# Six joints of a transformer block's kernel reordered, the recurrence's largest decays computed by ACT with the reference as bias, and one branch's matmuls dealt out along the last head

## The chip, the cores and the metric

The kernel runs on one core of one Trainium2 chip, in one launch. The metric is the device time of an execution in microseconds, as the median of several runs. A profile of one execution gives the start and duration of each instruction by engine: PE (TensorE, matmuls), PEld (its weight loads), DVE (VectorE), ACT (ScalarE), POOL (GpSimd) and SP (SyncE, which here issues transfers).

## The reference

One residual block on x of 1024 tokens by 1024 features, with 256 memory tokens:

```python
h = _rmsnorm(x, norm_mix_g[l])
z = h @ w_in[l]
(hq, hf, hi, hg, fq, fk, fv, ff, mq, gate_logits) = jnp.split(z, pts, axis=-1)
y_a = _hgrn2_mixer(hq, hf, hi, hg, ...)      # 4 heads, 128x128 state, recurrence over time
y_b = _fox_mixer(fq, fk, fv, ff, ...)        # 8 heads x 64, causal attention with forget bias
y_c = _memory_mixer(mq, mem_kv, ...)         # 4 heads x 128 into 256 memory tokens
gates = jax.nn.sigmoid(gate_logits)          # three gates per channel
merged = (gates[:, :, 0] * (y_a @ w_br_hgrn) + gates[:, :, 1] * (y_b @ w_br_fox)
          + gates[:, :, 2] * (y_c @ w_br_mem))
x = x + merged @ w_out
h2 = _rmsnorm(x, norm_ffn_g)
a, v = jnp.split(h2 @ w_up, 2, axis=-1)      # 2 x 2816 columns
x = x + (gelu(causal_dwconv3(a)) * v) @ w_down
```

The recurrence (HGRN2) of one head, with G the running sum of log f inside a block of the sequence:

```python
diff = Gc[:, :, :, None, :] - Gc[:, :, None, :, :]
decay = jnp.exp(jnp.where(causal, diff, -jnp.inf))
A = jnp.einsum('bhtc,bhsc,bhtsc->bhts', qc, kc, decay)
o = einsum('bhts,bhsv->bhtv', A, ic) + einsum('bhtc,bhcv->bhtv', qc * jnp.exp(Gc), S)
S_new = S * jnp.exp(G_last)[..., None] + einsum('bhsc,bhsv->bhcv', kc * jnp.exp(G_last - Gc), ic)
```

## The kernel before

**Matmuls.** Every fp32 product is made of three passes over operands that are split into a high part (a cast on ACT) and a low part (a subtraction on DVE): `mm3`, lines 114 to 116, high by high, high by low and low by high. Names end in h and l for the parts (wh and wl, gh and gl, dbh and dbl). The dense projections and the FFN's up projection use a scheme of seven products for a block of two by two, with one operand's sums in "families" (B11, T1, T2, B22, T3, B21, T4): `family_block` casts and subtracts one quarter of a family, and `product` multiplies 4 slices by 3 passes, 12 matmuls. In the FFN, `unit` does such a block of the up projection for one pair of weight chunks (o1 to o7 are its weight operands, `snap` copies a partial sum from PSUM to the tile fe), and `families` prepares the later families during the first unit.

**Order.** The kernel is written against a tile framework whose scheduler places the instructions of each engine in a list order. Generators are interleaved by weights (`weave`), a generator may run ahead at a higher priority (`ahead`), and `tc.issue_after(i)` forbids placing what stands in its block before the instruction i. PSUM tiles come from four tags: pp (three buffers), lg (two), tr (two) and po (one).

**Stages in order of time.** Start, with the memory's keys and values and the first gate weights (gh, gl), to about 57 us; the other first gates and dense projections to 235; the rest of attention's preparation and the memory's attention to 320; forgetting attention (fox) to 677; the recurrence (hgrn) to 917; the three branch projections to 1023; the output projection to 1110; the FFN's up projection to 1543; the down projection to the end.

**The start.** `differences` (line 536) scales the eight tiles xk by the norm's gain (line 542, ACT) and forms the sums of the families (line 545, DVE). Four of the eight scalings are held back behind `late["square"]`, the squares of the first norm.

**The recurrence.** `hgrn_prep(h)` projects head h: three chunks (values of q, decay and gate) of 48 matmuls in two column halves each, PSUM to the tile zt by a DVE product with the row norm rx (line 888), then tanh. `hgrn_mix(h)` has two halves of 512 tokens, four blocks of 128 in each. In a half, the matrix A of each block is filled in levels: the pairs (line 931, lg from qq and kt), then for H = 64, 32, 16, 8, 4, 2 the products between the two sides of a block of 2H tokens. For each level two DVE subtractions of a reference (G at the end of the left side) from G (lines 948 and 949), one exponential on ACT (line 950), one product with kt on POOL (line 951) and one with q on DVE (line 952) make the tile X, which PE multiplies (line 961 for H of 64 and 32, line 970 below), and a copy under a mask puts the result into A (line 972). Then kE, the decay to the end of a block, is made by a DVE subtraction, an ACT exponential and a DVE product (lines 980 to 982), transposed (line 990) and multiplied with the values (line 995). A and the state St give the output in po (lines 1001 and 1003), which is normed (o, rr), transposed (line 1022) and multiplied into ya (line 1023, DVE: the last instruction of a half).

Heads 0 to 2 are woven with the preparation of the next head. The last head is woven with six of the eight chunks of `branch(1)`, the fox branch's projection (its operands are yh and yl, its PSUM pp, 24 matmuls a chunk); the last two chunks are put behind the last matmul on A and St:

```python
weave((ahead(hgrn_mix(3, ya), AHEAD), HGRN_STEPS), (branch(1, yh, yl, range(6)), 12))
with tc.issue_after(state["last"].ins):
    run_all(branch(1, yh, yl, (6, 7)))
```

**The down projection** reads its weights (wr, from sd) and the up projection's result (br, from yd) in steps, casts and subtracts both (dwh, dwl, dbh, dbl), and begins with the quarter A11.

Of the kernel before, what the change touches and what calls it, by code (L numbers as in the profile page):

```python
# [14 lines left out]
P = 128  # L15
# [3 lines left out]
HB = 512  # L19
# [51 lines left out]
def tile_block(ctx: ExitStack, tc: tile.TileContext, xT, memT, x_rows, mem_rows, vec, fbias, mats, hmask, w_cm, w_hi, w_fqk, w_fv,  # L71
# [46 lines left out]
    def cast(eng, out, in_):  # L118
        if eng is S:
            S.copy(out, in_)  # L120
# [9 lines left out]
    def rstd_small(out, ss, n):  # L130
        w = ss.shape[1]
        V.tensor_scalar(out, ss, 1.0 / n, EPS, ALU.mult, ALU.add)
        G.tensor_tensor(out, out, mhalf[:, :w], ALU.pow)

# [401 lines left out]
    def differences():  # L536

        b = []
        for k in range(4):
            for t in (k, k + 4):  # L540
                with tc.issue_after(late["square"].ins) if t > 3 else nullcontext():
                    S.activation(xk[t], xk[t], AF.Copy, scale=col(C_GX + t))
# [333 lines left out]
    hset = {}  # L876

    def hgrn_prep(h):
        ph = state["ph"]
# [3 lines left out]
        for what, base, dst in ((0, 4, at), (1, 0, qt), (2, 8, gz)):  # L883

            for n, ps in cm_chunk(w_cm[base + h], KC, uh, ul, h == 3 and what == 2):
                sl = slice(n * HB, (n + 1) * HB)
                zt = ph.tile([P, HB], F32, tag="zt", name="zt")
                V.tensor_mul(zt, ps, rx[:, sl])  # L888
# [13 lines left out]
    def hgrn_mix(h, ya):  # L902
# [7 lines left out]
        for n in range(2):  # L910
# [16 lines left out]
            for d in range(2):  # L927
                pd = ps_lg()[:, :384].rearrange("p (b t) -> p b t", b=2)
                for b in range(2):
                    bb = 2 * d + b  # L930
                    PE.matmul(pd[:, b, :], kt[:, bb * P:(bb + 1) * P], qq[:, bb, :], start=True, stop=True)
                V.tensor_mul(A3[:, 2 * d:2 * d + 2, :], pd[:, :, 0:P], ident.unsqueeze(1).to_broadcast([P, 2, P]))
# [5 lines left out]
            for li, H in enumerate(LEVELS):  # L938
# [9 lines left out]
                V.tensor_sub(Xk, ref, Gv[:, :, 0, :])  # L948
                V.tensor_sub(Xq, Gv[:, :, 1, :], ref)
                S.activation(X, X, AF.Exp)  # L950
                G.tensor_mul(Xk, Xk, Kv[:, :, 0, :])  # L951
# [5 lines left out]
                if H >= 32:  # L957

                    for b in range(4):
                        bs = slice(b * 64, (b + 1) * 64)  # L960
                        PE.matmul(o[:64, bs], X[:, bs], X[:, 256 + b * 64:256 + (b + 1) * 64], start=True, stop=True)
                    A5 = A.rearrange("p (b j two h) -> p b j two h", b=4, two=2, h=H)
# [6 lines left out]
                for b in range(4):  # L969
                    PE.matmul(o[:, b * 64:(b + 1) * 64], X[:, b * P:(b + 1) * P],  # L970
                              Xq[:, b * bpb:(b + 1) * bpb, :], start=True, stop=True)
                V.copy_predicated(v4(A)[:, :, 1, :],
# [6 lines left out]
            kE = ph.tile([P, 4, P], F32, tag="kE", name="kE", bufs=2)  # L979
            V.tensor_sub(kE[:, :nb, :], G3[:, :nb, P - 1:P].to_broadcast([P, nb, P]), G3[:, :nb, :])  # L980
            S.activation(kE[:, :nb, :], kE[:, :nb, :], AF.Exp)
            V.tensor_mul(kE[:, :nb, :], kE[:, :nb, :], kt.rearrange("p (b t) -> p b t", b=4)[:, :nb, :])
# [33 lines left out]
            V.reduce_sum(rr, o2, axis=AX.X)  # L1016
            rstd_small(rr, rr, 4 * P)
            for b in range(4):
# [84 lines left out]
    for c in range(4):  # L1103
        for t, d in zip(yc, ycd):
            G.dma_start(t[c], d[:, c, :].bitcast(F32R))
    run_all(branch(0, yh, yl))
# [34 lines left out]
    def operand_parts(h, src):  # L1141
        l = pl.tile([P, HB], F32R, tag="wl2", name="wl2", bufs=5)
        late["split"] = split(S, h, l, src)
        return h, l
# [99 lines left out]

    def unit(src, put, begun=None, before=None, after=None):

# [5 lines left out]
        if begun:  # L1252
            x, y, e1, e5, e2, o4 = begun
            o5, o6, o7 = operand(sum_of(3, a11, a21)), operand(a12), operand(a22)
            before()
# [15 lines left out]
        if not begun:  # L1271
            o7 = operand(a22)
        z = ps_tr()
        product(z, o6, "B21", True)
# [36 lines left out]

    sums = weight_sums()

    for p in range(NF // 2):
# [123 lines left out]
    for a, b, own, first, c, n, sign, last, xq in (  # L1438
# [142 lines left out]
```

## Time and the profile before

| | us |
|---|---|
| median of three runs | 1764.69 (1764.61 to 1765.21) |
| the profiled execution | 1764.18 |
| its span in the profile | 1762.4 |
| PE busy | 1736.2 |
| DVE busy | 1185.8 |
| ACT busy | 786.7 |
| POOL busy | 334.7 |

The mean granted PE clock of the span is 0.996 of full speed. Times in a timeline are microseconds from the span's start: start, duration, engine, line, operation, output<-inputs, shape, and in brackets the idle time before it with what ended it. Matmuls overlap in the pipeline, so their durations add up to more than their starts are apart; the distance of starts is what one costs. Of a stretch, the share of time that PE was busy and the clock it was granted have to be read together.

### The profile page before, as it was taken

What the parts mean: (1) busy time and instruction counts of PE and PEld (TensorE: products, weight loads), DVE (VectorE), ACT (ScalarE), POOL (GpSimd) and SP (SyncE); (2) the same over time, 40 slices, a digit from 0 to 9 for tenths busy, and PEclk for the clock granted to TensorE, in tenths of its full rate; (3) what the DMA queues carried; (4) which work ended last, traced back from release to release, by engine and by line L of the source; (5) the groups of instructions that cost most, each with busy time, mean ns of one, the idle gap of its engine ahead of it and who ended that gap; (6) DMA issues with size and microseconds to landing.
All of it is one profiled execution on the core that took longest, in us unless ns stands there. A gap on an engine that the chain in (4) does not pass through costs nothing.

```text
span 1762.4 us, 24530 instructions
## 1 busy us (share of the span) xinstructions
PE 1736.2 (99%) x9069; PEld 1471.4 (83%) x9069; DVE 1185.8 (67%) x2181; ACT 786.7 (45%) x1318; POOL 334.7 (19%) x431
## 2 busy tenths in 40 slices
PE   8999999999999999999989999999999999999998
PEld 6778899989898997888878888788888888778887
DVE  7656445665756567778866755797777877674654
ACT  8633356545555554445331233543343443433332
POOL 1100032443424333334230000111111111100000
PEclk9999999999999999999999999999999999999999
DMA  9533232221212211001226452466454445494772
GB/s 361 178 119 105 83 128 73 76 95 60 91 47 85 84 46 52 25 31 56 77 78 216 153 200 80 136 188 163 139 160 133 119 128 152 144 362 145 238 269 84
DMA packets 83209, 227.36 MB, mean 129 GB/s; under 512 B 9600, under 2 KB 12424, under 8 KB 83088
## 3 DMA queue, kind: packets, MB, share of 16 engines
q1 hardware_dynamic: 65040, 161.29, 26.1%
q0 software_dynamic: 18048, 64.50, 12.6%
q8 instruction: 71, 1.16, 0.3%
q14 instruction: 50, 0.41, 0.1%
HBM read 180.88 MB, written 67.93 MB: 141 GB/s over the span
## 4 chain that ended last, share of the span: by engine, by line
PE 97%; ACT 1%; DVE 1%; DMA 0%; issue 0%; SPq 0%; POOL 0%; DVEq 0%; ACTq 0%
PE pp L115 21%; PE pp L116 21%; PE pp L114 21%; PE lg L115 4%; PE lg L116 4%; PE lg L114 4%; PE tr L114 2%; PE tr L115 2%; PE tr L116 2%; PE lg L970 2%; PE po L836 1%; PE lg L795 1%; PE lg L794 1%; PE po L835 1%; PE po L116 1%; PE po L114 1%
## 5 line engine op out<-in xcount | busy, mean ns | idle before, releaser
L115 PE MATMUL pp<-ul,wh 128*128 128x512 f32 x412 | 165.6, 402 | 0.0
L116 PE MATMUL pp<-uh,wl 128*128 128x512 f32 x412 | 165.4, 401 | 0.0
L114 PE MATMUL pp<-uh,wh 128*128 128x512 f32 x412 | 163.2, 396 | 1.5 <-DVE zt L888 1.5
L115 PE MATMUL pp<-wl,uh 128*128 128x256 f32 (+1 forms) x512 | 145.7, 285 | 0.0
L116 PE MATMUL pp<-wh,ul 128*128 128x256 f32 (+1 forms) x512 | 145.3, 284 | 0.0
L114 PE MATMUL pp<-wh,uh 128*128 128x256 f32 (+1 forms) x512 | 144.7, 284 | 0.0
L120 ACT CAST wh<-s 128x512 fp32r<-128x512 f32 x113 | 68.4, 619 | 152.8 <-PE pp L115 76.8
L120 ACT CAST wh<-raw 128x1024 fp32r<-128x1024 f32 (+2 forms) x76 | 67.5, 890 | 98.9 <-PE pp L115 86.9
L1250 POOL DMA_DIRECT2D rw<-in_w_up x44 | 24.1, 554 | 403.4 <-ACT sqs L1185 169.9
L114 PEld LDWEIGHTS pp<-wh,uh 128*128 128x128 f32 x512 | 96.4, 189 | 1.2
L116 PEld LDWEIGHTS pp<-wh,ul 128*128 128x128 f32 x512 | 96.5, 189 | 0.9
L115 PEld LDWEIGHTS pp<-wl,uh 128*128 128x128 f32 x512 | 96.4, 188 | 0.9
L120 ACT CAST dwh<-wr 128x1024 fp32r<-128x1024 f32 (+1 forms) x42 | 41.1, 980 | 124.6 <-PE tr L115 41.7
L120 ACT CAST wh<-rw 128x512 fp32r<-128x512 f32 x83 | 50.6, 619 | 101.2 <-PE pp L115 59.7
L114 PEld LDWEIGHTS pp<-uh,wh 128*128 128x128 f32 x412 | 78.4, 190 | 17.5 <-DVE zt L888 1.7
L115 PEld LDWEIGHTS pp<-ul,wh 128*128 128x128 f32 x412 | 77.9, 189 | 16.8
L116 PEld LDWEIGHTS pp<-uh,wl 128*128 128x128 f32 x412 | 77.9, 189 | 15.5
L128 DVE TENSOR_TENSOR wl<-raw,wh 128x1024 fp32r<-128x1024 f32 (+2 forms) x76 | 78.4, 1033 | 17.9 <-ACT wh L120 12.7
L128 DVE TENSOR_TENSOR wl<-s,wh 128x512 fp32r<-128x512 f32 x113 | 77.0, 683 | 8.9 <-ACT wh L120 8.9
L128 DVE TENSOR_TENSOR wl<-rw,wh 128x512 fp32r<-128x512 f32 x83 | 55.7, 686 | 29.5 <-PE pp L116 14.1
L951 POOL TENSOR_TENSOR X<-X,kt 128x256 f32<-128x256 f32 x48 | 50.4, 1057 | 124.5 <-ACT X L950 119.5
L128 DVE TENSOR_TENSOR dwl<-wr,dwh 128x1024 fp32r<-128x1024 f32 (+1 forms) x42 | 47.6, 1133 | 39.0 <-ACT dwh L120 39.0
(471 smaller groups left out, 5185.7 us busy)
## 6 DMA issues: line engine op xcount, KB each, us to landing
rw<-in_w_up POOLq DMA_DIRECT2D x44, 512.0 KB, 4.6
sd<-in_w_dn POOLq DMA_DIRECT2D x30, 512.0 KB, 5.9
br<-yd SPq DMA_DIRECT2D x30, 512.0 KB, 5.3
raw<-in_w_cm SPq DMA_DIRECT2D x26, 512.0 KB, 3.4
gd<-gt SPq DMA_DIRECT2D x48, 256.0 KB, 2.0
gt<-gd SPq DMA_DIRECT2D x48, 256.0 KB, 2.8
yd<-fc SPq DMA_DIRECT2D x44, 256.0 KB, 2.5
wr<-sd SPq DMA_DIRECT2D x20, 512.0 KB, 4.4
```

The lines of the kernel that those rows point to most:

```text
L114: PE.matmul(ps, lh, rh, start=first, stop=False, skip_group_check=more)
L115: PE.matmul(ps, lh, rl, start=False, stop=False, skip_group_check=more)
L116: PE.matmul(ps, ll, rh, start=False, stop=last, skip_group_check=more)
L120: S.copy(out, in_)
L128: return (sub or V).tensor_sub(l, src, h.bitcast(F32))
L794: PE.matmul(ps[:, :w], qa[i][:, tsl], kh[i][:, s0:s0 + w], start=True, stop=False)
L795: fox_sets[p][3] = PE.matmul(ps[:, :w], qa[i][:, tsl], kl[i][:, s0:s0 + w], start=False, stop=True)
L835: PE.matmul(o, vhl[:, sb, :], ph[:, src], start=(sb == 0), stop=False)
L836: PE.matmul(o, vhl[:, sb, :], pl[:, src], start=False, stop=last)
L951: G.tensor_mul(Xk, Xk, Kv[:, :, 0, :])
L970: PE.matmul(o[:, b * 64:(b + 1) * 64], X[:, b * P:(b + 1) * P], Xq[:, b * bpb:(b + 1) * bpb, :], start=True, stop=True)
L1250: late["raw"] = G.dma_start(raw[:, 2 * i:2 * i + 2, :], src[:, 2 * i:2 * i + 2, :])
```

## The change

1. All eight scalings of `differences` are held behind the squares, with the sums that need them.
2. In `hgrn_prep(0)` zt is a gate tile (a pool with three buffers, open all along) in place of the one buffer in the recurrence's own pool, which opens when attention's pool is released.
3. In `hgrn_mix`, at H = 64 the two subtractions and the exponential over 512 columns become one small ACT copy (nr, the negated reference, 128x4) and eight ACT exponentials over 64 columns with the reference as bias; kE's subtraction and exponential become four (or three) ACT exponentials over 128 columns with a bias. PE's steps of the recurrence are recorded in `state["at"]`, and `held` keeps each part of the fox branch's chunks 2 to 6 behind the third last of them. The last head's weave has other weights, and one chunk in place of two is left for the end.
4. The loads of yc (the memory branch's operands) come after the last norm of the recurrence.
5. In the FFN's first unit, the family B21 also waits for the cast of the weight operand o5, and T4 for that of o7.
6. The first step of A11 of the down projection (two slices) is loaded and split by `down_operands` inside the last up unit, before its products with B21 and T4, into weight buffers of the up projection.

```diff
-                with tc.issue_after(late["square"].ins) if t > 3 else nullcontext():
+                with tc.issue_after(late["square"].ins):
...
+    def held(gen, lag):
+        while True:
+            at = state["at"]
+            with tc.issue_after(at[-lag].ins) if len(at) >= lag else nullcontext():
+                try:
+                    next(gen)
+                except StopIteration:
+                    return
+            yield
...
-                zt = ph.tile([P, HB], F32, tag="zt", name="zt")
+                zt = ph.tile([P, HB], F32, tag="zt", name="zt") if h else gate_tile()
...
-                ref = Gv[:, :, 0, H - 1:H].to_broadcast([P, nb, H])
-                V.tensor_sub(Xk, ref, Gv[:, :, 0, :])
-                V.tensor_sub(Xq, Gv[:, :, 1, :], ref)
-                S.activation(X, X, AF.Exp)
+                if H == 64:
+                    nr = ph.tile([P, 4], F32, tag="nr", name="nr", bufs=2)
+                    S.activation(nr, Gv[:, :, 0, H - 1], AF.Copy, scale=-1.0)
+                    for b in range(nb):
+                        S.activation(Xk[:, b, :], Gv[:, b, 0, :], AF.Exp, bias=Gv[:, b, 0, H - 1:H], scale=-1.0)
+                        S.activation(Xq[:, b, :], Gv[:, b, 1, :], AF.Exp, bias=nr[:, b:b + 1])
+                else:
...
-            V.tensor_sub(kE[:, :nb, :], G3[:, :nb, P - 1:P].to_broadcast([P, nb, P]), G3[:, :nb, :])
-            S.activation(kE[:, :nb, :], kE[:, :nb, :], AF.Exp)
+            for b in range(nb):
+                S.activation(kE[:, b, :], G3[:, b, :], AF.Exp, bias=G3[:, b, P - 1:P], scale=-1.0)
...
-    weave((ahead(hgrn_mix(3, ya), AHEAD), HGRN_STEPS), (branch(1, yh, yl, range(6)), 12))
+    weave((ahead(hgrn_mix(3, ya), AHEAD), 18), (chain(branch(1, yh, yl, range(2)), held(branch(1, yh, yl, range(2, 7)), 3)), 14))
     with tc.issue_after(state["last"].ins):
-        run_all(branch(1, yh, yl, (6, 7)))
+        run_all(branch(1, yh, yl, (7,)))
...
+            with tc.issue_after(state["norm"].ins):
+                G.dma_start(t[c], d[:, c, :].bitcast(F32R))
...
+            o5 = operand(sum_of(3, a11, a21))
+            late["o5"] = late["cast"]
+            o6, o7 = operand(a12), operand(a22)
+            late["o7"] = late["cast"]
...
+                    order.enter_context(tc.issue_after(late["o7" if name == "T4" else "o5"].ins))
...
+    def down_operands():
+        raw = pw.tile([P, 4, HB], F32, tag="rw", name="rw", bufs=2)
+        G.dma_start(raw[:, 0:2, :], w_dn[:, 0, 0:2, :])
+        G.dma_start(raw[:, 2:4, :], yd[:, 0, 0:2, :])
+        ops = [operand(raw[:, i, :]) for i in (0, 2, 1, 3)]
+        late["down"] = [Blocks([ops[i + 2 * j][q] for j in range(2)]) for i in range(2) for q in range(2)]
...
-        unit(w_up[2 * p + 1], put_v, after=None if p else late["last"])
+        unit(w_up[2 * p + 1], put_v, after=None if p else late["last"],
+             ahead=down_operands if p == NF // 2 - 1 else None)
...
-            ops = [*parts("w", fetch("w", i, a, eng=eng)), *parts("b", yside(b, i, eng))]
+            if a == "A11" and i == 0:
+                ops = late["down"]
+            else:
+                ops = [*parts("w", fetch("w", i, a, eng=eng)), *parts("b", yside(b, i, eng))]
```

Three places show how the instructions move. The first is PE's list in the second half of the last head, before the change: X are the levels' tiles, o the normed output, kE and kT the decay to the block's end, Vf the values.

```order
L961 MATMUL lg<-X 64x64 x4
L1003 MATMUL po<-St,qe 128x128
L970 MATMUL lg<-X 128x64 x4
L961 MATMUL lg<-X 64x64 x4
L970 MATMUL lg<-X 128x64 x4
L1022 MATMUL tr<-ident,o_9129 128x128
L990 MATMUL tr<-ident,kE 128x128 x3
L970 MATMUL lg<-X 128x64 x4
L1022 MATMUL tr<-ident,o_9129 128x128 x3
L995 MATMUL tr<-Vf,kT 128x128 x3
L970 MATMUL lg<-X 128x64 x4
```

These rows are part of 26 with no projection between them. In the new order, the levels of the last head (line 995 is what 970 was, 984 what 961 was; yh and yl are the fox branch's operands) stand so:

```order
L995 MATMUL lg<-X 128x64 x4
L984 MATMUL lg<-X 64x64 x4
L114 MATMUL pp<-yh_8946,wh 128x512
L115 MATMUL pp<-yl_8950,wh 128x512
L116 MATMUL pp<-yh_8946,wl 128x512
L114 MATMUL pp<-yh_8947,wh 128x512
```

The branch's matmuls have moved in among the levels. The matmuls of `mm3` between one half's transpositions of o and the next half's were 91, 77, 83, 85, 86, 13 and 34 and are now 86, 65, 112, 24, 12, 72 and 64.

The second place is PE's list in the second half of the third head, as before the change (the branch's chunks already stand there):

```order
L970 MATMUL lg<-X 128x64 x4
L1022 MATMUL tr<-ident,o_8611 128x128
L990 MATMUL tr<-ident,kE 128x128 x3
L114 MATMUL pp<-yh_8893,wh 128x512
L115 MATMUL pp<-yl_8897,wh 128x512
L116 MATMUL pp<-yh_8893,wl 128x512
L114 MATMUL pp<-yh_8894,wh 128x512
L115 MATMUL pp<-yl_8898,wh 128x512
L116 MATMUL pp<-yh_8894,wl 128x512
L114 MATMUL pp<-yh_8895,wh 128x512
L1022 MATMUL tr<-ident,o_8611 128x128
```

and now (line 1048 is what 1022 was, 1016 what 990 was, 1021 what 995 was, 946 what 931 was):

```order
L995 MATMUL lg<-X 128x64 x4
L984 MATMUL lg<-X 64x64 x4
L1048 MATMUL tr<-ident,o_8654 128x128
L1016 MATMUL tr<-ident,kE 128x128 x3
L1048 MATMUL tr<-ident,o_8654 128x128 x3
L995 MATMUL lg<-X 128x64 x4
L1021 MATMUL tr<-Vf,kT 128x128 x3
L995 MATMUL lg<-X 128x64 x4
L946 MATMUL lg<-qq,kt 128x192 x2
L995 MATMUL lg<-X 128x64 x4
L946 MATMUL lg<-qq,kt 128x192 x2
```

The branch's matmuls have left this place; the rows are part of 26 without a projection.

The third place is ACT's list in the first unit of the FFN, before (wh from s is the cast of o5's high part, B21h and T4h those of the families):

```order
L1215 COPY fe<-pp 128x512
L120 CAST B21h<-x_4_10251 128x512
L120 CAST B21h<-x_5_10252 128x512
L120 CAST B21h<-x_6_10253 128x512
L120 CAST B21h<-x_7_10254 128x512
L120 CAST T4h<-x_0_10247 128x512
L120 CAST T4h<-x_1_10248 128x512
L120 CAST T4h<-x_2_10249 128x512
L120 CAST T4h<-x_3_10250 128x512
L120 CAST wh_10928<-s_10926 128x512
```

and now:

```order
L1243 COPY fe<-pp 128x512
L120 CAST wh_10996<-s_10994 128x512
L120 CAST B21h<-x_4_10319 128x512
L120 CAST B21h<-x_5_10320 128x512
L120 CAST B21h<-x_6_10321 128x512
L120 CAST B21h<-x_7_10322 128x512
L120 CAST wh_11000<-rw 128x512
L120 CAST wh_11004<-rw 128x512
L120 CAST T4h<-x_0_10315 128x512
```

The weight's cast has moved ahead of both families, and two more weight casts ahead of T4.

More of the change, by code (lines that the diff above doesn't have):

```diff
@@ L119, in cast @@
         if eng is S:
-            S.copy(out, in_)
+            return S.copy(out, in_)
         elif eng is V:
@@ L132, in rstd_small @@
         V.tensor_scalar(out, ss, 1.0 / n, EPS, ALU.mult, ALU.add)
-        G.tensor_tensor(out, out, mhalf[:, :w], ALU.pow)
+        return G.tensor_tensor(out, out, mhalf[:, :w], ALU.pow)
     wsplit = [S, V]
@@ L876, in tile_block, with step @@
     hset = {}
+    def step(ins):
+        state.setdefault("at", []).append(ins)
+    def held(gen, lag):
[7 more added lines that the diff above has]
+            yield
     def hgrn_prep(h):
@@ L930, in hgrn_mix @@
                     bb = 2 * d + b
-                    PE.matmul(pd[:, b, :], kt[:, bb * P:(bb + 1) * P], qq[:, bb, :], start=True, stop=True)
+                    step(PE.matmul(pd[:, b, :], kt[:, bb * P:(bb + 1) * P], qq[:, bb, :], start=True, stop=True))
                 V.tensor_mul(A3[:, 2 * d:2 * d + 2, :], pd[:, :, 0:P], ident.unsqueeze(1).to_broadcast([P, 2, P]))
@@ L946, in hgrn_mix @@
                     Xk, Xq = v4(X)[:, :, 0, :], v4(X)[:, :, 1, :]
[L947 to L950 removed]
+                if H == 64:
[5 more added lines that the diff above has]
+                else:
+                    ref = Gv[:, :, 0, H - 1:H].to_broadcast([P, nb, H])
+                    V.tensor_sub(Xk, ref, Gv[:, :, 0, :])
+                    V.tensor_sub(Xq, Gv[:, :, 1, :], ref)
+                    S.activation(X, X, AF.Exp)
                 G.tensor_mul(Xk, Xk, Kv[:, :, 0, :])
@@ L960, in hgrn_mix @@
                         bs = slice(b * 64, (b + 1) * 64)
-                        PE.matmul(o[:64, bs], X[:, bs], X[:, 256 + b * 64:256 + (b + 1) * 64], start=True, stop=True)
+                        mm = PE.matmul(o[:64, bs], X[:, bs], X[:, 256 + b * 64:256 + (b + 1) * 64],
+                                       start=True, stop=True)
+                    step(mm)
                     A5 = A.rearrange("p (b j two h) -> p b j two h", b=4, two=2, h=H)
@@ L969, in hgrn_mix @@
                 for b in range(4):
-                    PE.matmul(o[:, b * 64:(b + 1) * 64], X[:, b * P:(b + 1) * P],
-                              Xq[:, b * bpb:(b + 1) * bpb, :], start=True, stop=True)
+                    mm = PE.matmul(o[:, b * 64:(b + 1) * 64], X[:, b * P:(b + 1) * P],
+                                   Xq[:, b * bpb:(b + 1) * bpb, :], start=True, stop=True)
+                step(mm)
                 V.copy_predicated(v4(A)[:, :, 1, :],
@@ L1142, in operand_parts @@
         l = pl.tile([P, HB], F32R, tag="wl2", name="wl2", bufs=5)
-        late["split"] = split(S, h, l, src)
+        late["cast"] = cast(S, h, src)
+        late["split"] = V.tensor_sub(l, src, h.bitcast(F32))
         return h, l
@@ L1243, in sum_of, with unit @@
         return t
-    def unit(src, put, begun=None, before=None, after=None):
+    def unit(src, put, begun=None, before=None, after=None, ahead=None):
         raw = pw.tile([P, 4, HB], F32, tag="rw", name="rw", bufs=2)
@@ L1272, in unit @@
             o7 = operand(a22)
+        if ahead:
+            ahead()
         z = ps_tr()
@@ L1312, in tile_block, with __init__, __getitem__ @@
     sums = weight_sums()
+    class Blocks:
+        def __init__(self, tiles):
+            self.tiles = tiles
+        def __getitem__(self, at):
+            return self.tiles[at[1]][:, at[2]]
+    def down_operands():
[4 more added lines that the diff above has]
+        late["down"] = [Blocks([ops[i + 2 * j][q] for j in range(2)]) for i in range(2) for q in range(2)]
     for p in range(NF // 2):
```

4 lines of the change are left out of this document (1 added, 3 removed).

## The prediction

> **What bounds the kernel now.** I read the page first: the busy shares, then the chain that ended last.
>
> ```profile
> span 1762.4 us, 24530 instructions
> PE 1736.2 (99%) x9069; PEld 1471.4 (83%) x9069; DVE 1185.8 (67%) x2181; ACT 786.7 (45%) x1318; POOL 334.7 (19%) x431
> PE 97%; ACT 1%; DVE 1%; DMA 0%; issue 0%; SPq 0%; POOL 0%; DVEq 0%; ACTq 0%
> ```
>
> PE is busy for 1736.2 of 1762.4 us, so everything that is not matmul is 26.2 us, and the chain is PE for 97%. The change removes no matmul. It can gain only where PE stands still or is granted a lower clock, and it can lose wherever a new order makes PE wait. So the second view is what PE waits for (us in total, times, longest):
>
> ```profile
> PE lg L970 <- POOL X L951: 4.5, 1, 4.5
> PE pp L114 <- ACT wh L120: 2.6, 1, 2.6
> PE pp L115 <- DVE dbl L128: 1.5, 1, 1.5
> PE pp L114 <- DVE zt L888: 1.5, 1, 1.5
> ```
>
> Each happens once: these are joints between stages, and each edit of the change is aimed at one of them. The third view, busy time by stretch, shows what a joint costs beyond its idle time (PE, PEld, DVE, ACT, POOL busy with counts, granted PE clock, DMA share, GB/s):
>
> ```profile
> 678.00:682.00 4.00, 3.80 (x10) 2.98 (x11) 1.90 (x4) 1.26 (x2) 3.08 (x2) 0.57 0.48 143
> 861.90:890.80 28.90, 28.90 (x168) 24.84 (x167) 22.06 (x49) 8.86 (x19) 7.96 (x8) 1.00 0.40 119
> 895.50:917.50 22.00, 16.48 (x117) 15.71 (x115) 15.88 (x39) 6.30 (x14) 7.14 (x6) 0.84 0.11 37
> 1538.00:1546.00 8.00, 5.82 (x23) 3.84 (x22) 6.80 (x9) 4.84 (x5) 0.89 (x2) 0.96 1.02 332
> 1546.00:1549.00 3.00, 3.00 (x9) 2.37 (x8) 3.00 (x4) 0.00 (x0) 1.25 (x3) 0.55 0.99 380
> ```
>
> At 861.9 PE is busy without a gap at full clock while DVE is at 22.06 of 28.90 us: with projections between its steps the recurrence costs PE nothing. At 895.5, where none are left, PE idles 22.00 − 16.48 = 5.5 us, and the clock of 0.84 takes 22.00 × 0.16 = 3.5 us more. After the joints at 678 and 1546 the clock falls too, which costs 4.00 × 0.43 = 1.7 us and 8.00 × 0.04 + 3.00 × 0.45 = 1.7 us.
>
> **The change part by part.** The sum is made against the profiled execution, 1764.18 us, which is 0.51 under the median of 1764.69.
>
> Joint 1, the start. The second gate weights are cast late, behind a scaling of xk that nobody needs yet:
>
> ```profile
> 23.96 1.14 ACT L542 ACTIVATE xk<-xk,cv 128x1024 f32<-128x1024 f32 x1
> 25.00 1.03 ACT L120 CAST gh<-raw 128x1024 fp32r<-128x1024 f32 x1
> ...
> 26.08 0.51 PE L114 MATMUL po<-uh,gh 128*128 128x512 f32 x1 [1.35 <-ACT gh L120]
> 27.34 0.50 PE L116 MATMUL po<-uh,gl 128*128 128x512 f32 x1 [0.53 <-DVE gl L128]
> ...
> 13.84 0.33 SPq L139 DMA_DIRECT2D raw<-in_w_cm  x1
> ...
> raw<-in_w_cm SPq DMA_DIRECT2D x1, 512.0 KB, 9.1
> ```
>
> The weights land at 13.84 + 9.1 = 22.9, so with the scalings gone the cast ends near 22.9 + 1.03 = 24.0, ahead of PE's arrival at 26.08 − 1.35 = 24.7. The waits, 1.35 + 0.53 = 1.9, go; I take 1.8. If another ACT instruction slips ahead of the cast, only 0.5 goes, so 0.5 to 1.9. The four moved scalings (1.1 us each on ACT, their four DVE differences with them) now run under the gate matmuls behind the squares, where PE has a queue of work; without that cover they would cost up to 1 us where the first sum of families is multiplied. The later yc loads (joint 4) are priced at nothing: no wait of PE names them, and branch 0's matmuls stand between their landing and their use.
>
> Joint 2, from attention to recurrence. The one zt buffer made PE wait, since the pool that holds it opens only when attention's is released:
>
> ```profile
> 673.15 0.33 PE L823 MATMUL tr<-ident,pt 128*128 128x128 f32 x1 [0.59 <-DVE pl L128]
> 675.56 0.39 PE L836 MATMUL po<-pl,vhl 128*128 128x256 f32 x1 [0.34 <-DVE pl L128]
> 678.20 0.72 PE L114 MATMUL pp<-uh,wh 128*128 128x512 f32 x1 [1.51 <-DVE zt L888]
> ```
>
> With a gate tile from a pool of three, 66 projection matmuls of head 0 move in among attention's last steps. They cover 0.59 + 0.34 + 1.51 = 2.4 us of idle time, and with it the clock's 1.7 us: gain 4.1. The lower end, 2.4, holds if the clock falls anyway. The price is that the first recurrence step comes later by those matmuls, which nobody waits for.
>
> The clock needs a word, since 6.9 us of the sum hang on it (1.7, 3.5 and 1.7). The rows show it at about half behind an idle time of 1.51 us. The Trainium skill ("TensorE: Matmul & The Clock Gate", Part 1) has the clock fall only after an idle window of about 3.4 us; by that alone joints 2 and 6 would have no clock time to give back and the sum would be 3.4 us smaller. The trace does not agree with it for gaps of 1.5 us, and its numbers decide.
>
> Joint 3, the recurrence's end. Two things change. First the decays of level 64 and of kE. The rows of the dry stretch:
>
> ```profile
> 902.63 0.62 ACT L950 ACTIVATE X<-X 128x512 f32<-128x512 f32 x1
> 903.15 0.51 ACT L981 ACTIVATE kE<-kE 128x384 f32<-128x384 f32 x1
> 908.76 1.14 ACT L1019 ACTIVATE o<-po,rr 128x128 f32<-128x128 f32 x4 [2.84 <-POOL rr L133]
> 4.15 0.19 ACT L249 ACTIVATE lbe<-lbe 128x4 f32<-128x4 f32 x1
> ...
> 903.24 0.40 DVE L948 TENSOR_TENSOR X<-Gt 128x256 f32<-128x256 f32 x1
> 902.17 0.54 DVE L980 TENSOR_TENSOR kE<-Gt 128x384 f32<-128x384 f32 x1
> ```
>
> DVE loses 2 × 0.40 + 0.54 = 1.3 us a half. ACT loses 0.62 + 0.51 = 1.1 us and gains one tiny copy (0.19), eight exponentials of 64 and three or four of 128. Four of 128 take 1.14, so 0.285 each; one of 64 lies between 0.19 and 0.285. That is 0.19 + 1.5 to 2.3 + 0.9 to 1.1, about 3 us: ACT is up by 1.5 to 2.5 us a half. ACT was busy 6.30 of 22.00 us even in the dry stretch, so I price it at nothing there, and the rest is rival D. The Trainium skill ("ScalarE: Activation LUTs", What ACT_TABLE_LOAD costs) speaks against this edit: 280 ns fixed with a bias taken per partition, plus 0.833 ns an element, less 93 ns of overlap. Estimated from that page, eight of 64 take 1.9 us, inside my bounds; its 0.293 for 128 agrees with the row's 0.285.
>
> Second, the fox branch's matmuls are dealt out along the last head. Before, the last half but one had 13 of them and went at the pace of the recurrence's own steps:
>
> ```profile
> 891.43 0.75 DVE L1023 SCALAR_TENSOR_TENSOR ya<-tr,hgc,hz 128x512 f32<-128x512 f32 x1 [2.40 <-PE tr L1022]
> ...
> 912.89 0.74 DVE L1023 SCALAR_TENSOR_TENSOR ya<-tr,hgc,hz 128x512 f32<-128x512 f32 x1
> ...
> 907.63 1.97 PE L970 MATMUL lg<-X 128*128 128x64 f32 x8 [4.55 <-POOL X L951]
> ...
> 903.33 4.25 POOL L951 TENSOR_TENSOR X<-X,kt 128x256 f32<-128x256 f32 x2 [2.36 <-ACT X L950]
> ```
>
> From one ya to the next it took 21.5 us. PE waited 4.55 us for a product that POOL made in a pair lasting 4.25 us. Now the last head's two halves have 72 and 64 such matmuls, so this stretch, 5.5 + 3.5 = 9.0 us of loss, is covered. But the cover comes from somewhere: in the new order the third head's last half and the half after it hold 24 and 12 matmuls, and 26 rows without one stand there, as many as before and of the same kinds. What that stretch costs no row shows. If the nearest row holds, 9.0. DVE has 1.3 us a half less in it, about 2 over one and a half halves, which gives 7. If both halves kept the 21.5 us of before, which with the removed subtractions is about 20 each, 40 us stand against PE work of 2 × 8.4 (22.0 − 9.0 = 13.0 for one and a half halves' steps gives 8.7, and the gapless stretch a little less) plus 36 matmuls of 0.23, together 25: a loss of up to 14. If POOL's pair does not fall on the same place and DVE runs ahead, 0. Near the stretch itself I take 8.0: the joint gains 9.0 − 8.0 = 1.0, between −5.0 and 9.0. It is the widest term.
>
> Joint 5, the first FFN unit. PE waits for a weight cast that stands behind eight casts of families on ACT:
>
> ```profile
> 1118.27 2.18 ACT L120 CAST B21h<-x 128x512 fp32r<-128x512 f32 x4
> 1120.35 2.17 ACT L120 CAST T4h<-x 128x512 fp32r<-128x512 f32 x4
> 1122.43 0.62 ACT L120 CAST wh<-s 128x512 fp32r<-128x512 f32 x1
> ...
> 1123.10 0.50 PE L114 MATMUL pp<-T3h,wh 128*128 128x512 f32 x1 [2.60 <-ACT wh L120]
> ```
>
> In the new order the cast takes the place at 1118.27 where B21's begin, and is done by 1118.9, before PE's 1123.10 − 2.60 = 1120.5. The 2.6 us go. B21's casts begin 0.6 us later and T4's by three weight casts later, at most 1.9 us, and PE has T3's 12 matmuls in front of B21's and B21's 12 in front of T4's, 2.8 us each at the 0.23 us below. If DVE's share of the split comes late, 1.5 goes: 1.5 to 2.6.
>
> Joint 6, from up to down. The first operands of the down projection are split while PE waits:
>
> ```profile
> 1539.33 0.50 PE L114 MATMUL pp<-T4h,wh 128*128 128x512 f32 x1 [0.32 <-DVE fe L1362]
> 1541.73 0.39 PE L115 MATMUL pp<-T4l,wh 128*128 128x512 f32 x1
> 1541.96 0.39 PE L116 MATMUL pp<-T4h,wl 128*128 128x512 f32 x1
> ...
> 1543.13 0.50 PE L114 MATMUL pp<-dbh,dwh 128*128 128x512 f32 x1 [0.33 <-DVE fc L1365]
> 1545.40 0.79 PE L115 MATMUL pp<-dbl,dwh 128*128 128x512 f32 x1 [1.53 <-DVE dbl L128]
> ```
>
> A matmul starts every 0.23 us. Now 24 matmuls of the down projection, 5.5 us of work, stand on operands that were loaded and split inside the last up unit: 12 about T3 and 12 after T4. They cover 0.32 + 0.33 + 1.53 = 2.2 us, and the clock's 1.7 us go with it: 3.8, at least 2.2. Next is the split of the second step, which has 2.8 us of these matmuls as its cover; without it about 1.5 us would come back.
>
> Sum: 1.8 + 4.1 + 1.0 + 2.6 + 3.8 = 13.3, so 1764.18 − 13.3 = 1750.9, and with 0.51 to the median **1751.4 us**. With every term at its ends the gain is 1.6 to 21.4.
>
> **The rivals.** A is the forecast: the dry stretch, one head earlier, costs 5 to 11 us; 1748 to 1754.
>
> B: it costs more than 11 us and the joints give their lower ends. For it: DVE's 21.5 us a half and two thin halves in a row where there was one. Against it: DVE has less to do. Gain 4 to 10, 1754.5 to 1760.5; I price it at 1757. A part of it, 0.04, is that joints 2 and 6 lose their idle time but had no clock time to give back: 1751.4 + 3.4 = 1754.8. (The clock gate's rule, above, would have it so.)
>
> C: the stretch costs under 5 us, since DVE and POOL run ahead or the clock stays up. For it: the 4.55 us are one single wait, behind one slow pair on POOL. Against it: 16.48 us of PE work in 22.0. Gain 16.4 to 21.4, so 1743.3 to 1748.3; priced at 1745.
>
> D, slower: ACT becomes the recurrence's bound. The narrow exponentials stand in order in front of those of the lower levels, so each half's chain is longer by ACT's 1.5 to 2.5 us, in eight halves 12 to 20. It decides from (12.3 + 3.5) / 8 = 2.0 us a half on PE's path (12.3 is what the other four joints give). At 2.5 us the time is 1764.69 − 12.3 + 20 = 1772. For it: PE waits for X. Against it: at 861.9 ACT is busy 8.86 of 28.90 us and PE has no gap.
>
> E: no difference. The loads of joint 6 land late, gate_tile is not free and joint 3 costs its lower end, so that less than 3.5 us is left: 1763.
>
> **How the numbers follow.** A 0.50, B 0.23, C 0.16, D 0.06, E 0.05. I predict A's 1751.4. For 8 in 10 the range takes A, all of B but its worst tenth and C but its last microsecond: 1744.5 to 1759.5. About 0.2%, 3.5 us, is what a measurement of this kernel can tell from no change. A, B and C are faster by more than that: 0.89. E is same: 0.05. D is slower: 0.06.
>
> **What would show it.** In the changed kernel's waits the rows on zt, dbl and wh should be gone, the clock at attention's end and at the change to the down projection should be full, and gh should be cast right after landing. A stretch 30 to 60 us before the recurrence's end should have PE idle on X or A, with a clock under 1. I am wrong on joint 3 if that stretch has no idle time (C) or over 11 us of loss (B), and on the whole if PE waits on ACT's X in every half (D).

## The result, and the profile after

The changed kernel takes 1767.91 us (median of 15 runs, 1764.78 to 1770.91) against 1765.21 us before (15 runs, 1761.57 to 1769.4): the ratio is 1.0014, with an interval of 1.0004 to 1.0024. That is slower by less than the 0.2% named above, where 13.3 us faster was forecast; the case of no difference had 0.05. The profiled execution took 1765.08 us, the second fastest of the 15 runs, so its profile shows less loss than a typical run had. Its page, the lines that answer to those of before:

```profile
span 1763.3 us, 24584 instructions
PE 1738.2 (99%) x9069; PEld 1472.5 (84%) x9069; DVE 1172.4 (66%) x2159; ACT 803.9 (46%) x1404; POOL 339.6 (19%) x431
PE 93%; DVE 3%; DMA 2%; issue 1%; POOL 1%; ACT 1%; SPq 0%; DVEq 0%; POOLq 0%; ACTq 0%
```

DVE has 13 us less to do and ACT 17 more; over eight halves the prediction's figures make about 10 less and 12 to 20 more. PE's idle time is 1763.3 − 1738.2 = 25.1 us after 26.2: hardly anything closed. PE's waits (us, times, longest), behind the one for the first weights at the very start (5.4 now, 5.8 before), tell that it moved:

```profile
PE tr L1048 <- ACT o L1045: 5.2, 2, 3.4
PE pp L116 <- DVE fa L1370: 1.6, 1, 1.6
PE lg L995 <- DVE A L948: 1.5, 1, 1.5
PE lg L995 <- POOL X L974: 1.2, 1, 1.2
PE pp L114 <- ACT fe L427: 1.2, 1, 1.2
```

The rows on zt, dbl and on the 2.6 us weight cast are gone, as forecast. In their place stand, of those shown, three rows of the recurrence's steps (lines 995 and 1048), one in the FFN and a larger one at line 427 (0.7 before). By stretch:

```profile
675.00:705.00 30.00, 30.00 (x151) 25.27 (x150) 16.51 (x27) 14.71 (x28) 8.10 (x6) 1.00 0.26 83
840.00:890.00 50.00, 40.73 (x238) 35.28 (x237) 41.99 (x92) 23.30 (x64) 22.86 (x21) 0.83 0.14 43
867.50:877.40 9.90, 9.38 (x38) 9.19 (x39) 5.77 (x14) 2.65 (x9) 3.31 (x4) 0.50 0.01 2
895.50:917.50 22.00, 22.00 (x133) 18.81 (x132) 16.07 (x35) 7.17 (x17) 5.93 (x5) 1.00 0.34 96
1540.00:1552.00 12.00, 12.00 (x54) 9.77 (x53) 8.86 (x14) 8.98 (x10) 0.01 (x1) 1.00 0.83 305
```

Attention's end, the last head and the change to the down projection run without a gap at full clock. But 840 to 890, the third head's second half and what follows, loses 9.3 us of idle time and 50.00 × 0.17 = 8.5 us of clock: 17.8, where the old dry stretch lost 9.0. Such a sum counts a little twice, since PE is idle for part of the time at half clock (3.3 us from 863 to 880): with the clock charged to PE's busy time alone the stretch loses 16.1. The largest wait:

```profile
862.15 3.06 POOL L133 TENSOR_TENSOR rr<-rr,mhalf 128x4 f32<-128x4 f32 x1 [3.45 <-DVE rr L132]
...
865.24 1.14 ACT L1045 ACTIVATE o<-po,rr 128x128 f32<-128x128 f32 x4 [1.79 <-POOL rr L133]
...
865.66 0.48 PE L1048 MATMUL tr<-ident,o 128*128 128x128 f32 x1 [3.41 <-ACT o L1045]
```

The norm of a half goes through a power of 128x4 values on POOL, which took 3.06 us here (1.01 to 1.87 us in the recurrence of the kernel before; why POOL was slower here is not shown). PE has the transpositions of o next in its list and nothing to put before them.

### The profile page after: what moved, and what is told of

Its sections match the earlier page's. It is cut to its first block, busy times and chain, and to the rows that moved or that the text cites. A ratio compares the mean times of both kernels' runs of the same rounds, so it can differ in the third digit from the quotient of the medians.

```text
span 1763.3 us, 24584 instructions
## 1 busy us (share of the span) xinstructions
PE 1738.2 (99%) x9069; PEld 1472.5 (84%) x9069; DVE 1172.4 (66%) x2159; ACT 803.9 (46%) x1404; POOL 339.6 (19%) x431
## 4 chain that ended last, share of the span: by engine, by line
PE 93%; DVE 3%; DMA 2%; issue 1%; POOL 1%; ACT 1%; SPq 0%; DVEq 0%; POOLq 0%; ACTq 0%
PE pp L116 20%; PE pp L115 20%; PE pp L114 20%; PE lg L116 4%; PE lg L115 4%; PE lg L114 4%; PE tr L115 2%; PE tr L114 2%; PE tr L116 2%; PE lg L995 2%; PE po L836 1%; PE lg L795 1%; PE lg L794 1%; PE po L835 1%; PE po L116 1%; PE po L114 1%
## 5 line engine op out<-in xcount | busy, mean ns | idle before, releaser
L115 PEld LDWEIGHTS pp<-ul,wh 128*128 128x128 f32 x412 | 77.5, 188 | 16.1
L810 ACT ACTIVATE pt<-pt,st 128x128 f32<-128x128 f32 (+3 forms) x64 | 49.7, 777 | 39.6 <-DVE st L807 32.9
L812 POOL TENSOR_SCALAR pt<-pt,st 128x128 f32<-128x128 f32 (+3 forms) x64 | 51.8, 810 | 77.6 <-DVE st L811 60.7
```

The source lines that it names most:

```text
L115: PE.matmul(ps, lh, rl, start=False, stop=False, skip_group_check=more)
L810: S.activation(pt[:, :ns], pt[:, :ns], AF.Exp, bias=st[:, 2:3], accum_out=st[:, 3:4])
L812: G.tensor_scalar(pt[:, :ns], pt[:, :ns], st[:, 3:4], 0.0, ALU.mult, ALU.add)
```

## The experiments

Two theories on where the gain went were open at first. S: the deal of the fox branch stripped the third head of cover. E: the narrow exponentials lengthen each half.

**Three undoings.** e1 takes back the last head's weave, e2 the narrow exponentials, e3 both:

```diff
-    weave((ahead(hgrn_mix(3, ya), AHEAD), 18), (chain(branch(1, yh, yl, range(2)), held(branch(1, yh, yl, range(2, 7)), 3)), 14))
+    weave((ahead(hgrn_mix(3, ya), AHEAD), HGRN_STEPS), (branch(1, yh, yl, range(6)), 12))   # e1, e3 (and two chunks at the end)
-                    S.activation(Xk[:, b, :], Gv[:, b, 0, :], AF.Exp, bias=Gv[:, b, 0, H - 1:H], scale=-1.0)
+                V.tensor_sub(Xk, ref, Gv[:, :, 0, :])                                           # e2, e3 (Xq and kE likewise)
```

> The changed kernel with the last head woven as before (six chunks of the fox branch free to move, two at the end); the narrow exponentials and the other joints stay. Theory S (the third head's last halves were stripped of cover by the deal, and that stretch loses 18 us in idle time and clock): the stretch at 840 to 890 us is gone, a dry stretch returns at the last head's second half and loses 9 to 12 us, the time is 1756 to 1760. Rival E (the narrow exponentials lengthen every half's chain): the loss stays where the exponentials are, 1765 or more.

> The changed kernel with the decays of level 64 and of kE made as before (DVE subtraction, one ACT exponential); the deal and the other joints stay. S: the third head's halves are still thin (24 and 29 projection matmuls) and lose about as much, 12 to 18 us; 1763 to 1769. E: the loss in the recurrence goes, 1754 to 1758.

> The changed kernel without the deal and without the narrow exponentials: only the start, zt's tile, the loads of yc, the FFN's first unit and the down projection's first operands. S: its dry stretch is in the last head as before and loses 9 to 12; the other joints are worth about 8 by the two profiles (4.1 and 3.9 at zt and at the down projection, 1 in the FFN, nothing net at the start), so 1756 to 1760, and equal to the kernel with only the deal undone. E: 1754 to 1758, and clearly below that kernel.

Measured: e1 1772.5 (ratio to the kernel before in the same round 1.0027, interval 1.0013 to 1.0042; so for every run below), e2 1768.0 (1.0010, 1.0000 to 1.0020), e3 1768.71 (1.0014, 1.0003 to 1.0025). e1 lies where E put it, e2 where S put it, and e3 in neither range, so neither theory holds. Neither undoing helps, and the joints alone are slower than before, though the recurrence's code in e3 is that of before but for zt. In e3's order the intervals between the halves hold 107, 70, 71, 106, 14, 0 and 34 projection matmuls where before held 91, 77, 83, 85, 86, 13 and 34. This points at something ahead of the recurrence that uses up its cover, the projections that PE can do between its steps.

**Cover by hand.** e4 keeps the projections of heads 2 and 3 back too:

```diff
-        weave((ahead(hgrn_mix(h, ya), AHEAD), HGRN_STEPS), (hgrn_prep(h + 1), 6))
+        weave((ahead(hgrn_mix(h, ya), AHEAD), HGRN_STEPS), (held(hgrn_prep(h + 1), 3) if h else hgrn_prep(h + 1), 6))
```

> The changed kernel with one edit more: the projections of heads 2 and 3 are kept behind the third last step of the recurrence as well, so that the intervals between the halves hold 48, 70, 68, 54, 84, 72 and 85 projection matmuls and none is thin. S: the recurrence loses 0 to 4 us where the changed kernel loses 18, so 1749 to 1755. E: the chain of each half is as long as in the changed kernel, and the waits spread over the halves, 1762 or more.

Measured 1764.46 (0.9989, 0.9978 to 1.0000): 3.5 us better than the changed kernel, far from S's range and in E's, which e2 speaks against. With cover spread evenly, PE waits at 740 and 845 us instead. That suggests too little cover in all.

**Theory Z: zt's gate tile.** Attention's last matmul (line 836), the recurrence's first step (line 931, now 946) and what leads up to it, in the kernel before:

```profile
676.42 0.28 PE L836 MATMUL po<-pl,vhl 128*128 128x128 f32 x1
690.05 1.46 PE L931 MATMUL lg<-qq,kt 128*128 128x192 f32 x8
...
678.18 0.63 ACT L890 ACTIVATE ha<-zt 128x512 f32<-128x512 f32 x1 [1.08 <-DVE zt L888]
...
678.92 3.99 POOL L893 TENSOR_SCALAR ha<-ha,c 128x512 f32<-128x512 f32 x2 [10.82 <-ACT ha L890]
...
685.24 0.87 DVE L923 SCALAR_TENSOR_TENSOR qq<-ha,c,hq 128x256 f32<-128x256 f32 x1
```

and in the changed kernel:

```profile
690.09 0.28 PE L836 MATMUL po<-pl,vhl 128*128 128x128 f32 x1
703.56 1.46 PE L946 MATMUL lg<-qq,kt 128*128 128x192 f32 x8
...
690.41 0.37 ACT L839 COPY yp<-po 64x256 f32<-64x256 f32 x1 [5.71 <-PE po L836]
690.68 1.15 ACT L905 ACTIVATE ha<-gt 128x512 f32<-128x512 f32 x2
...
691.41 3.99 POOL L908 TENSOR_SCALAR ha<-ha,c 128x512 f32<-128x512 f32 x2 [19.88 <-ACT ha L905]
...
698.73 0.48 DVE L938 SCALAR_TENSOR_TENSOR qq<-ha,c,hq 128x256 f32<-128x256 f32 x1
```

In both kernels the first step comes about 13.5 us after attention's last matmul (690.05 − 676.42 = 13.6; 703.56 − 690.09 = 13.5). The first 9 to 10 us of this are a chain off PE: tanh into ha begins just behind attention's last copy, then come POOL for 4 us and qq, the step's last operand, done at 686.1 and now at 699.2. For the last 4 us PE has projections in its list ahead of the step. By the code, ha lies in the recurrence's own pool, as zt did, and only zt was moved out of it. The gate tile let projections of head 0 run before attention's end, which came 13.7 us later for them; the chain did not begin earlier. In these 13.5 us PE takes 57 projection matmuls now, by the trace the last 20 of head 0 and the first 37 of head 1, where it took 44 of head 0 before. What is taken ahead of the first step is missing behind it. e5 takes the gate tile out of e3, e6 puts it alone into the kernel before:

```diff
-                zt = ph.tile([P, HB], F32, tag="zt", name="zt") if h else gate_tile()
+                zt = ph.tile([P, HB], F32, tag="zt", name="zt")          # e5; e6 is the reverse, in the kernel before
```

> The kernel with only the start, the loads of yc, the FFN's first unit and the down projection's first operands changed (the joints alone, without zt's gate tile). Theory Z (zt's gate tile lets 66 projections of head 0 run under attention, so that the recurrence's first step comes 13.5 us later and that much cover is missing at its end): without it the recurrence's order is that of before again, its dry stretch loses about 9 us, and the down projection and the FFN give about 5: 1759 to 1762. Rival F (these joints give nothing by themselves, since the clock's windows only fall elsewhere): 1764 to 1768.

> The kernel before with zt's gate tile alone. Z: attention's end has no idle time and a full clock (4.1 us gained), but the intervals between the recurrence's halves become 107, 70, 71, 106, 14, 0 and 34 projection matmuls and the dry stretch loses about 18 us instead of 9: 1768 to 1773. Rival (the joint gives what it shows, and the dry stretch grew for another reason): 1760 to 1763.

Measured, with the kernel before at 1765.91 in this round: e5 1760.67 (0.9973, 0.9961 to 0.9985), in Z's range, and e6 1774.43 (1.0045, 1.0027 to 1.0062), 1.4 us above it. The rivals' ranges hold neither, so Z stands in its direction, with a price larger than it said: alone, the gate tile costs 8.5 us, and the other joints alone gain 5.2. e6 by stretch:

```profile
670.00:700.00 30.00, 30.00 (x153) 25.22 (x152) 13.16 (x22) 10.65 (x17) 7.11 (x6) 1.00 0.18 55
890.00:925.00 35.00, 25.56 (x162) 24.91 (x161) 27.39 (x64) 12.44 (x28) 10.91 (x12) 0.76 0.01 1
```

The joint at 678 is closed exactly as meant, and 9.4 us of idle time and 8.4 of clock stand 220 us later. Against the 9.0 that the old dry stretch lost and the 4.1 that the joint gave, these 17.8 make 4.7 us net; e6's profiled run, the fastest of its six, is 6.2 us above the profiled run of before. The rest of the 8.5 is in no stretch that was looked at.

**The changed kernel without zt's gate tile,** the same one line taken back:

> The changed kernel without zt's gate tile alone; deal, narrow exponentials and the other joints stay. Theory Z (cover brought ahead of the recurrence's first step is missing at its end): the intervals hold 100, 94, 86, 83, 27, 83 and 53 projection matmuls, one thin half in place of two, so the recurrence loses 5 to 9 us where the changed kernel lost 19, and attention's end waits 2.4 us again with 1.7 of clock: 1757 to 1762. Rival D (the deal of the fox branch strips the third head, with or without zt): 1766 or more.

Measured 1755.34 (0.9936, 0.9919 to 0.9953; 1755.24 to 1756.20), 12.6 us under the changed kernel and the lowest median of all. It is faster than either range: the rival that the deal strips the third head with or without the gate tile (called D there, not the prediction's D) is out, and the loss that Z still expected is mostly not there. Its stretches:

```profile
676.00:682.00 6.00, 4.16 (x26) 3.53 (x26) 3.22 (x6) 2.34 (x5) 0.93 (x1) 1.00 0.16 33
840.00:890.00 50.00, 48.34 (x295) 41.36 (x294) 45.02 (x93) 25.39 (x62) 16.52 (x17) 1.00 0.25 82
895.50:917.50 22.00, 22.00 (x132) 18.62 (x130) 13.50 (x28) 6.66 (x16) 4.06 (x4) 1.00 0.31 101
```

The 1.8 us at 676 are back; 840 to 890 loses 1.7 us where the changed kernel lost 17.8.

**What each part is worth without the gate tile.** From e9, e13 takes the narrow exponentials out, e14 the deal, e15 the start's edit (the diffs above; for e15 the `if t > 3` is put back):

> The changed kernel without zt's gate tile and with DVE's subtractions in place of the narrow exponentials; the deal stays. Intervals 91, 77, 83, 85, 15, 81, 55. If the deal is what joint 3 gains (the dry place is covered), 1755 to 1758. If the exponentials are (the chain and DVE relieved), the thin interval of 15 loses 5 to 9 us with its clock: 1760 to 1765.

> The changed kernel without zt's gate tile and with the last head woven as before; the narrow exponentials stay. Intervals 100, 94, 86, 83, 85, 26 and 33, with 40 PE instructions without a projection in the last head as before. If the deal is what joint 3 gains, 1759 to 1762, with a dry stretch of 7 to 10 us at the recurrence's end. If the exponentials are, 1755 to 1757.

> The changed kernel without zt's gate tile and with the start as before. Intervals 104, 89, 86, 75, 36, 83 and 53, nearly the same as with the start's edit. If the edit is worth the 1.8 us forecast, 1756.5 to 1758; if its gain at 26 us comes back as waits at 90 and 235 us, 1754.5 to 1756.

Measured: e13 1758.1 (0.9958, 0.9944 to 0.9972), e14 1765.62 (1.0001, 0.9991 to 1.0010), e15 1757.3 (0.9953, 0.9939 to 0.9967). e13 is 0.1 us above the range in which the deal is the gain, and e15 is in the range of 1.8 us for the start. The two edits of joint 3 hang together. With the exponentials the deal gains 10.3 us (e14 to e9); without them the medians are 2.6 apart (e5 to e13), but the intervals overlap. e14 is slower than both of its ranges, and slower than e5, which has neither edit. Its stretch and its largest wait there:

```profile
895.00:930.00 35.00, 29.23 (x161) 26.49 (x161) 19.68 (x45) 9.91 (x25) 10.32 (x12) 0.80 0.17 49
...
PE tr L1048 <- ACT o L1045: 5.0, 1, 5.0
```

5.8 us idle and 7.0 of clock stand at the recurrence's end, where e9 has 0.2 and none, so it is the deal that covers this place. It does not tell e14 from e5, which loses 5.5 and 7.0 from 895 to 930; why e14 is the slower one stays open. With the deal, e9 is 2.8 us under e13, but the intervals overlap, and the same holds for e15's 2.0: what the exponentials and the start are worth is not settled.

**Even cover without the gate tile.** e7 (no exponentials, lag 5), e8 (with them), e10 (lag 7), e11 (lag 6, the gate tile for the first column half alone) and e12 (e8 with the start as before) hold all heads' projections back by the edit of e4, with `held(hgrn_prep(h + 1), lag)` for every h:

```diff
+                zt = ph.tile([P, HB], F32, tag="zt", name="zt") if not (h == 0 and what == 0 and n == 0) else gate_tile()   # e11
```

> The changed kernel without zt's gate tile and without the narrow exponentials, with all heads' projections kept behind the fifth last step of the recurrence: 71, 65, 83, 75, 81, 64 and 55 projection matmuls between the halves, and no 40 PE instructions with fewer than 19. Z: no stretch of the recurrence loses more than 2 us, 9 less than before, and the other joints give 5: 1750 to 1755. Rival (POOL's norm or DVE bound the halves whatever the cover): 1758 or more.

> The same with the narrow exponentials: 91, 72, 83, 54, 79, 78 and 58 between the halves, one place of 40 instructions with 14. If these cost nothing where cover is even, within 3 us of the kernel without them; if they lengthen each half's chain, 5 or more us above it.

> The even kernel with the narrow exponentials, the projections kept behind the seventh last step: 100, 86, 72, 71, 61, 81 and 55, no 40 PE instructions with fewer than 18 (14 before). If cover alone sets the loss, the recurrence loses 0 to 3 us where the even kernel of lag 5 lost 5.6, and the time is 1755 to 1759; if POOL or DVE set single waits whatever the cover, 1759 to 1762.

> The even kernel (lag 6) with the gate tile for the first column half of head 0's projections alone: some 24 matmuls go under attention's end, more than its 2.4 us of idle time need, and the recurrence starts later by those only. If cover is only moved, the gain at attention's end (up to 4.1 us) is kept and about half of what zt's tile cost comes back: 1755 to 1760. If any cover taken there is paid in full, 1760 to 1764.

> The even kernel (lag 5, narrow exponentials) with the start as before: four scalings free to go early. By the profiles the start's edit takes 1 to 2 us out of the first 57 us and puts about as much in as new waits at 80 to 100 and at 235 us. If that is its effect, the waits at 26 us are back, those at 90 and 235 are 1 to 2 us smaller, and the time is within 2 us of the even kernel with it. If the edit is worth its 1.8 us, it is 1.5 to 2 slower.

Measured: e7 1764.91 (0.9989, 0.9978 to 1.0001), e8 1759.07 (0.9959, 0.9945 to 0.9973), e10 1759.67 (0.9958, 0.9943 to 0.9974), e11 1761.13 (0.9971, 0.9959 to 0.9982), e12 1760.47 (0.9962, 0.9947 to 0.9977). All medians are above e9, whose projections lie less evenly. For e7 and e11 the intervals are apart from e9's; of e10 and e12, measured in the same round as e9, no run is as fast as e9's slowest; e8's interval overlaps. So even cover was not better, and e7 is no support for Z: it fell in its rival's range (POOL or DVE bound the halves whatever the cover). PE waits 7.0 us in e7's recurrence, all for DVE, and 2.9 in e8's, which is most of the 5.0 between the two profiles; that the removed subtractions make this difference is argued, not shown, and neither of e8's forecasts had it 5.8 us below e7. e10 also fell in the range of its rival, and e12 cannot be told from e8. e11 fell in the range in which cover taken ahead of the first step is paid in full, but its interval overlaps those of e8 and e10, which take none.

## Why the prediction was wrong

**Joint 2 is the step that failed.** The prediction wrote: "The price is that the first recurrence step comes later by those matmuls, which nobody waits for." The joint gave what was forecast in its place, 2.4 us of idle time and the clock. But the step came about 13.5 us behind attention's end as before, most of it a chain that the gate tile does not shorten, so the matmuls taken early are missing at the recurrence's end, where projections are the scarce thing. The prediction itself had shown, at 861.9 against 895.5, that the recurrence costs nothing with projections and 9.0 us without; it did not count that matmuls used up ahead of the first step are missing inside: 585 stand between the first step and the last half's norm instead of 638, although the deal brings a chunk of 24 more; with the gate tile alone (e6) 567. Put at −8.5 (alone) or −12.6 (in this kernel) instead of 4.1, joint 2 decides the sign: from the kernel before over e5 and e9 to the changed one the steps are 5.2 us faster, 5.3 faster and 12.6 slower.

**Joint 3** was forecast at 1.0 with a loss of 8.0 in the new dry stretch, at most 14. In this kernel it lost 17.8 by the same reckoning, so the bound was too narrow; it left the clock out, and its own 40 − 25 is 15. I priced one dry stretch by the old one's row. It came with two thin halves (24 and 12 projections) and with half a clock for 17 us in place of 6.8. Without the gate tile, deal and exponentials together gain 5.3 (e5 to e9). The fear of rival B was right on the mechanism; where the cover had gone was not known to it.

**The other joints** together were forecast at 8.2 and gave 5.2 (e5). Joint 6 came out as forecast between the two profiles: no gap and full clock at 1540, 2.2 and 1.7. Only the first is the joint's own: in e6, where the old gap stands, the clock stays full there (1548 to 1556: 1.86 us idle, clock 1.00). Joint 1 gave less than 1.8 in the profile, and at 88 and 236 us larger or new waits stand:

```profile
24.32 0.49 PE L114 MATMUL po<-uh,gh 128*128 128x512 f32 x1 [0.29 <-ACT gh L120]
25.57 0.50 PE L116 MATMUL po<-uh,gl 128*128 128x512 f32 x1 [0.54 <-DVE gl L128]
88.05 0.51 PE L114 MATMUL pp<-T2h,wh 128*128 128x512 f32 x1 [1.21 <-ACT fe L427]
236.76 1.05 PE L655 MATMUL tr<-ones,msq 128*128 128x1 f32 x8 [0.75 <-ACT msq L652]
```

1.88 became 0.83, and 0.68 at 88 became 1.21, as in each profile with this edit that was compared; in e12 and e15, without it, the old values are back. The wait at 236 is not the edit's alone: e6 has it without the edit (0.8), and e13 has the edit and not the wait. In all, PE's idle time fell by 1.5 us up to 57 us and rose by 1.4 from there to 235, so the profile leaves nearly nothing of the 1.8. Joint 5 was mis-sized, 1.0 for 2.6: the wait on the cast is gone, and a new one comes in the next unit.

```profile
1124.69 0.62 ACT L120 CAST wh<-s 128x512 fp32r<-128x512 f32 x1
...
1128.31 0.69 DVE L1270 TENSOR_TENSOR s<-rw 128x512 f32<-128x512 f32 x1 [2.23 <-DMA rw<-in_w_up]
...
1136.28 0.50 PE L116 MATMUL pp<-B11h,wl 128*128 128x512 f32 x1 [1.58 <-DVE fa L1370]
```

The cast moved up as forecast. DVE then stands 2.23 us on the next weights, with B21's and T4's subtractions queued behind; that this is what makes fa late is argued, not shown. The new wait stands in e3, e5 and e9 too, and not in e6, which lacks the edit.

**Right** was the price of the narrow exponentials on ACT, and in the changed kernel the rejection of rival D:

```profile
846.90 0.33 ACT L968 ACTIVATE X<-Gt,nr 128x64 f32<-128x64 f32 x1
847.14 0.33 ACT L967 ACTIVATE X<-Gt 128x64 f32<-128x64 f32 x1
```

They start 0.24 us apart, inside the bounds of 0.19 and 0.285. (The estimate from the Trainium skill, "ScalarE: Activation LUTs", What ACT_TABLE_LOAD costs, was 0.24: the trace agrees.) PE waits on ACT's X nowhere in the changed kernel, and without the exponentials it takes as long (e2, 1768.0). Where the deal is missing, the kernels that have them are the slower ones, e14 by 4.9 us than e5 and e1 by 3.8 than e3 (there the intervals overlap): less than D's 12 to 20, and why stays open.

## What to carry to other kernels

A gap that is filled with work from a later stage is not closed but moved, if that stage is short of that work: ask what the borrowed instructions covered, and whether the later stage's first step really comes earlier. Here one line that closed a 2.4 us gap cleanly cost 8 to 13 us, 200 us later. And undo edits one at a time as well as doing them alone: with the other parts undone first, the culprit stayed in every kernel.

## What the runs showed of the hardware

The clock time that the prediction added to a gap is not tied to the gap. At the same joint with the same waits, 2.4 us in all, the clock fell in the kernel before (0.57 for 4 us) and stayed full in e5:

```profile
676.00:682.00 6.00, 4.01 (x31) 3.42 (x29) 3.56 (x7) 2.98 (x6) 0.00 (x0) 1.00 0.05 11
```

Where it falls, it stays at half for multiples of about 3.4 us: 3.4 at 678, 6.8 at 907 and 3.4 at 1545 in the kernel before, 17.1 from 863 to 880 in the changed one, although PE was busy 9.38 of 9.90 us within that time with matmuls of 64 to 192 columns (the 867.50 row above). The Trainium skill ("TensorE: Matmul & The Clock Gate", Part 1) has a window of 3.4 us that runs free of the kernel; the multiples agree with it, and a gap that brings the half clock in one kernel and not in another fits it. The same part of the Trainium skill's page ("TensorE: Matmul & The Clock Gate", Part 1) has one busy window bring the clock back; these 17.1 us do not agree with that. How long a kernel runs at half clock changes from run to run, and with it the time: the 15 runs of the changed kernel have mean granted clocks from 0.995 at 1765.08 us to 0.992 at 1770.91, 1763 × 0.003 = 5.3 us, while e9's five runs have 0.999 to 1.000 and lie within 1 us.
